# Stick-breaking attention in parts: the running product is turned itself and meets differences of values

## The chip, the cores and the metric

The kernel runs on one core of a Trainium2 chip. Its engines are TensorE (PE in the profile, with its weight loads as PEld), VectorE (DVE), ScalarE (ACT), GpSimd (POOL) and SyncE (SP), which here only issues DMAs. Each engine takes its instructions in the order in which they were written for it and waits at the first one that is not ready. The metric is the device time of one execution in microseconds, as the median over runs.

## The reference

One decoder layer on 2048 tokens of 1024 channels, all in float32: a norm; one input projection to conv value, conv gate, q, k and v; a causal depthwise convolution of width 31 with gate, norm and swish; stick-breaking attention of 8 heads of 64 channels with a norm per head; an output projection; a residual; and a gated feed-forward part. The change touches attention alone. Cut to what it computes:

```python
z = einsum("bhqd,bhkd->bhqk", q, k) / 8
mask = key_pos < q_pos                       # strictly earlier tokens
log_beta = log_sigmoid(z)
log_1m_beta = where(mask, log_sigmoid(-z), 0)
between = cumsum(log_1m_beta, reverse=True) - log_1m_beta
attn = where(mask, exp(log_beta + between), 0)
out = attn @ v
```

Written without logarithms, token t gives to an earlier token s the weight sigmoid(z_ts) times the product of sigmoid(-z_tj) over all j between s and t. Let R_s be the product over all j from s up to the token just before t. Then, as sigmoid(z) = 1 - sigmoid(-z), the weight of s is R_(s+1) - R_s, with R_t = 1.

## The kernel before

**Precision.** A float32 operand is split into a high half (the value rounded to the fast matmul type, written by ACT) and a low half (the rest, a subtraction on DVE or POOL), and a product is two or three matmuls of halves. A "low half" below is such a subtraction (`split`, L592 to L595).

**Stages.** Tokens go in four groups g of 512 (`G`). A list `PLAN` (L40) orders the main stream of PE: input projection of groups 0 to 3 (L602 to L606), output projections (L1030 to L1032) as groups become ready, and the first parts of the feed-forward work (`c11`, `p4`, L1104). Beside this stream run three side streams, each reaching a share of its work at a given point of the main stream: attention, the convolution (31 taps a channel block on DVE, L820) and sums of feed-forward weights on POOL (L1188). When all of these are written, a planner (`Graph`) replaces the written order: it models every instruction with a cost and every buffer with its users, orders each engine's instructions anew, and pins that order. What follows, from about 1460 us on, is the rest of the feed-forward part; it is ordered separately.

**V.** The projection of v for one pair of heads leaves PSUM through ACT into a tile vs, channels by tokens (L777). After the next projection PE turns it in four blocks (L782), the halves are made, and the result goes to DRAM (`vd`). q and k go to DRAM as halves.

**Attention.** A unit is one head and one group of 512 keys; a head of group g has g + 1 units, from the newest keys to the oldest. A unit has four row blocks j of 128 queries. For each, `scores` does this:

- PE: z = QK, two matmuls (L904, L905), into one of two PSUM banks;
- on the newest (diagonal) unit, whose width is (j + 1) x 128, DVE adds -1e30 above the diagonal (L907, 128 x 128);
- POOL copies the carry of the unit before, one column, to the end of tile om (L909), and ACT writes sigmoid(-z) beside it (L910);
- ACT writes sigmoid(z) to tile A (L912);
- DVE replaces om by its running product from right to left, carry first (L914, one element more than the keys);
- POOL multiplies A by om shifted by one (L915), and copies the last product to pv, the next carry (L917).

The scan's second operand is a broadcast that it does not use; it is a column of z in PSUM, except in the last group's heads 4 to 7 (`late`), where it is a column of ones in SBUF.

`values` then takes the unit before the current one, one key block of 128 at a time: PE turns the four row blocks of A (L931), ACT and DVE make the halves TH and TL, and PE adds V times both to the head's sum o (L936, L937). At a head's end ACT copies o to oT (L1001); three quarter-units later PE turns it and DVE adds the two halves (`fold_halves`, L952, L953), and every second head the pair is normalised and turned back (`back`, L969).

Buffers: om has four, A six, z and the turned blocks (at) two PSUM banks each, o and oT one.

## Time and profile before

| | us |
|---|---|
| median of 3 runs | 2450.47 |
| lowest and highest run | 2440.8, 2454.69 |
| the profiled execution, whole | 2447.04 |
| its span, first to last instruction | 2445.3 |

The profile is of one execution. A row of a group of instructions reads: line, engine, operation, output from inputs, shape, count | busy us in all, mean ns of one | idle time of the engine just before them, and what ended most of it. A row of a wait reads: who waited, for whom, us in total, times, longest. A row of a stretch of time gives its length and then, for each engine, busy us and the number of instructions. The first scan starts at 62.2 us and the last one ends before 1380 us, so all that the change touches lies in the first 1400 us. The granted clock of TensorE is 0.993 of full speed over the span.

### The profile page before, as it was taken

What the parts mean: (1) busy time and instruction counts of PE and PEld (TensorE: products, weight loads), DVE (VectorE), ACT (ScalarE), POOL (GpSimd) and SP (SyncE); (2) the same over time, 40 slices, a digit from 0 to 9 for tenths busy, and PEclk for the clock granted to TensorE, in tenths of its full rate; (3) what the DMA queues carried; (4) which work ended last, traced back from release to release, by engine and by line L of the source; (5) the groups of instructions that cost most, each with busy time, mean ns of one, the idle gap of its engine ahead of it and who ended that gap; (6) DMA issues with size and microseconds to landing.
All of it is one profiled execution on the core that took longest, in us unless ns stands there. A gap on an engine that the chain in (4) does not pass through costs nothing. (4 is left out here: it accounts for less than half of the span.)

```text
span 2445.3 us, 35497 instructions
## 1 busy us (share of the span) xinstructions
PE 2360.7 (97%) x11156; PEld 1927.7 (79%) x11156; DVE 1786.1 (73%) x2305; ACT 1295.6 (53%) x2398; POOL 1528.3 (62%) x1845
## 2 busy tenths in 40 slices
PE   8999999999999999998899999999999999999998
PEld 6788887787878777886678877777888887887886
DVE  6997999999997899766751257677656664556656
ACT  4567675776666655666664653333323235454543
POOL 5756477674767667669941147754766665567656
PEclk9999999999999999999999999999999999999999
DMA  9898876888699799875598769878888777668765
GB/s 317 282 317 270 278 233 227 294 282 256 224 298 312 247 340 323 299 258 177 197 339 276 264 223 330 307 263 274 291 293 277 261 253 252 198 190 277 240 192 177
DMA packets 279197, 648.40 MB, mean 265 GB/s; under 512 B 34400, under 2 KB 34400, under 8 KB 279008
## 3 DMA queue, kind: packets, MB, share of 16 engines
q1 hardware_dynamic: 263168, 617.29, 75.6%
q10 hardware_dynamic: 15840, 28.84, 3.1%
q8 instruction: 88, 1.44, 0.2%
q14 instruction: 101, 0.83, 0.1%
HBM read 456.21 MB, written 189.79 MB: 264 GB/s over the span
## 5 line engine op out<-in xcount | busy, mean ns | idle before, releaser
L915 POOL TENSOR_TENSOR A<-A,om 128x512 f32<-128x512 f32 (+2 forms) x320 | 326.8, 1023 | 332.7 <-DVE om L914 249.3
L1398 POOL TENSOR_TENSOR wL<-raw,wH 128x512 fp32r<-128x512 f32 x176 | 254.5, 1469 | 196.5 <-ACT wH L1397 165.4
L820 DVE SCALAR_TENSOR_TENSOR cv<-glu,cw,cv 128x512 f32<-128x512 f32 x464 | 346.8, 747 | 4.7
L1629 DVE TENSOR_TENSOR xL__21922<-t__21924,xH__21921 128x512 fp32r<-128x512 f32 x154 | 198.3, 1293 | 160.7 <-ACT xH__21921 L1628 160.4
L1627 POOL TENSOR_TENSOR xL__21920<-t__21923,xH__21919 128x512 fp32r<-128x512 f32 x154 | 212.0, 1383 | 155.9 <-ACT xH__21919 L1626 152.3
L914 DVE TENSOR_TENSOR_SCAN om<-om,one,z 128x513 f32<-128x513 f32 (+3 forms) x256 | 278.3, 1100 | 16.6 <-ACT A L912 13.6
L595 DVE TENSOR_TENSOR TL<-at,TH 128x512 fp32r<-128x512 f32 (+1 forms) x320 | 188.6, 600 | 122.9 <-ACT TH L594 120.6
L602 PE MATMUL inps<-xH,wL 128*128 128x512 f32 x640 | 258.4, 404 | 3.7 <-ACT sg L769 2.6
L604 PE MATMUL inps<-xH,wH 128*128 128x512 f32 x640 | 256.2, 401 | 0.0
L606 PE MATMUL inps<-xL,wH 128*128 128x512 f32 x640 | 256.1, 400 | 0.0
L1104 PE MATMUL dps<-xH__21919,xL__21922 128*128 128x512 f32 x616 | 240.9, 391 | 3.5 <-DVE xL__21922 L1629 2.7
L1104 PE MATMUL dps<-xL__21920,xH__21921 128*128 128x512 f32 x616 | 240.6, 391 | 1.8 <-POOL xL__21920 L1627 1.8
L1104 PE MATMUL dps<-xH__21919,xH__21921 128*128 128x512 f32 x616 | 240.3, 390 | 0.0
L910 ACT ACTIVATE om<-z 128x512 f32<-128x512 f32 (+2 forms) x320 | 173.1, 543 | 111.5 <-DVE z L907 59.2
L556 ACT ACTIVATE wH<-raw 128x1024 fp32r<-128x1024 f32 x156 | 166.6, 1068 | 117.3 <-PE inps L606 50.3
L931 PE MATMUL at<-idr,A 128*128 128x128 f32 x1088 | 198.2, 274 | 16.0 <-POOL A L915 12.1
L1626 ACT ACTIVATE xH__21919<-t__21923 128x512 fp32r<-128x512 f32 x154 | 97.3, 632 | 217.7 <-POOL xL__21920 L1627 120.2
L594 ACT ACTIVATE TH<-at 128x512 fp32r<-128x512 f32 (+1 forms) x320 | 168.3, 544 | 74.5 <-PE at L931 69.3
L1397 ACT ACTIVATE wH<-raw 128x512 fp32r<-128x512 f32 x176 | 101.2, 623 | 172.5 <-PE b L1104 56.2
L931 PEld LDWEIGHTS at<-idr,A 128*128 128x128 f32 x1088 | 140.1, 140 | 58.2 <-POOL A L915 16.5
L912 ACT ACTIVATE A<-z 128x512 f32<-128x512 f32 (+2 forms) x320 | 173.1, 544 | 17.1 <-PE at L931 17.1
L560 POOL TENSOR_TENSOR wL<-raw,wH 128x1024 fp32r<-128x1024 f32 x50 | 121.3, 2428 | 48.9 <-ACT wH L556 33.5
(292 smaller groups left out, 6324.8 us busy)
## 6 DMA issues: line engine op xcount, KB each, us to landing
wL<-wL SPq DMA_DIRECT2D x156, 512.0 KB, 5.3
raw<-in_w_in_dram SPq DMA_DIRECT2D x80, 512.0 KB, 5.7
t__21924<-u SPq DMA_DIRECT2D x154, 256.0 KB, 2.8
c<-c ACTq DMA_DIRECT2D x88, 256.0 KB, 4.8
t__21923<-wd SPq DMA_DIRECT2D x88, 256.0 KB, 2.9
K<-kd SPq DMA_DIRECT2D x80, 256.0 KB, 4.3
V<-vd SPq DMA_DIRECT2D x80, 256.0 KB, 4.5
u<-accf SPq DMA_DIRECT2D x22, 768.0 KB, 4.8
```

The lines of the kernel that those rows point to most:

```text
L595: nc.vector.tensor_tensor(L, ps, H.bitcast(F32), ALU.subtract)
L602: nc.tensor.matmul(ps, WL[:, kc], aH[t](k), start=k == 0, stop=False)
L604: nc.tensor.matmul(ps, WH[:, kc], aH[t](k), start=False, stop=False)
L606: nc.tensor.matmul(ps, WH[:, kc], aL[t](k), start=False, stop=k == KT - 1)
L820: nc.vector.scalar_tensor_tensor(to, gl[c][:, k:k + G], cw[:, c, k:k + 1], a, ALU.mult, ALU.add)
L914: nc.vector.tensor_tensor_scan(r, r, (one if late else z[:, 0:1]).to_broadcast([P, w + 1]), one, ALU.mult, ALU.bypass)
L915: nc.gpsimd.tensor_tensor(a[:, 0:w], a[:, 0:w], om[:, G - w + 1:G + 1], ALU.mult)
L931: nc.tensor.transpose(pt[:, j * P:(j + 1) * P], u["A"][j][:, b * P:(b + 1) * P], id32)
L1104: return nc.tensor.matmul(ps, a, b, skip_group_check=True, **flags)
L1398: nc.gpsimd.tensor_tensor(l, t, f32(h), sub)
L1627: nc.gpsimd.tensor_tensor(WL, w, f32(WH), sub)
L1629: nc.vector.tensor_tensor(UL, t, f32(UH), sub)
```

## The change

The weights R_(s+1) - R_s are not formed. The sum over s of (R_(s+1) - R_s) v_s is regrouped as the sum over s of R_s (v_(s-1) - v_s), plus v_(t-1). So:

- **scores.** om gets sigmoid(-z) alone, and the scan's running product R is what PE turns later. A, its sigmoid and its multiplication are gone, as are both copies of carries: the scan takes its start value from column 0 of the om tile of the unit before.
- **diagonal.** The mask is gone. The diagonal scan computes (mark + state) x om from right to left with start 0, where `lower` has a single 1 in each row, at the token just before the query: the state stays 0 until there and is the product from there on. Its operands are two SBUF tensors. For row 0 of row block 0 that token lies in the key group before, so for groups 1 to 3 POOL adds the mark to that block's carry (L923 in the new kernel).
- **values.** Unchanged, but the V that is read is the difference of neighbours: POOL makes `step` from vs (one subtraction of 511 columns, one of a single column against the last column of the group before, one copy of that column), and PE turns `step` instead of vs. vs also goes to DRAM, by SP (16 stores of 256 KB).
- **head's end.** v_(t-1) is loaded back for a pair of heads (16 loads) and POOL adds its 64 channels to oT, in either half of the partitions, before the folding.
- **buffers.** om has eight, A none.

```diff
+    lower = ap.tile([P, G], F32, name="lower", bufs=1)
+    nc.gpsimd.memset(lower, 0.0)
+    nc.gpsimd.affine_select(lower, lower, pattern=[[1, G]], compare_op=ALU.not_equal, fill=1.0, base=P + 1 - G,
                             channel_multiplier=-1)
+    vlast = cc.tile([P, 48], F32, name="vlast")
+    nc.gpsimd.memset(vlast, 0.0)
...
                 nc.scalar.activation(vs, ps, AF.Copy)
-
-                def later(c=c, vs=vs):
+                nc.sync.dma_start(vsd[c][:, g * G + 1:(g + 1) * G + 1], vs)
+                step = ev("step")
+                nc.gpsimd.tensor_tensor(step[:, 1:G], vs[:, 0:G - 1], vs[:, 1:G], ALU.subtract)
+                nc.gpsimd.tensor_tensor(step[:, 0:1], vlast[:, c:c + 1], vs[:, 0:1], ALU.subtract)
+                nc.gpsimd.tensor_copy(vlast[:, c:c + 1], vs[:, G - 1:G])
+
+                def later(c=c, vs=step):
...
-            return dict(QH=QH, QL=QL, prev=[one] * TT, o=None)
+            return dict(QH=QH, QL=QL, prev=[lower[:, 0:1]] * TT, o=None)
...
+            om = ap.tile([P, G], F32, tag="om", name="om", bufs=NOM)
+            nc.scalar.activation(om[:, 0:w], z[:, 0:w], AF.Sigmoid, scale=-0.125)
+            r = om[:, 0:w][:, ::-1]
             if diag:
-                nc.vector.tensor_tensor(z[:, w - P:w], z[:, w - P:w], msk, ALU.add)
-            om = ap.tile([P, G + 9], F32, tag="om", name="om", bufs=NOM)
-            nc.gpsimd.tensor_copy(om[:, G:G + 1], hd_["prev"][j])
-            nc.scalar.activation(om[:, G - w:G], z[:, 0:w], AF.Sigmoid, scale=-0.125)
-            a = ap.tile([P, G], F32, tag="A", name="A", bufs=NA)
-            nc.scalar.activation(a[:, 0:w], z[:, 0:w], AF.Sigmoid, scale=0.125)
-            r = om[:, G - w:G + 1][:, ::-1]
-            nc.vector.tensor_tensor_scan(r, r, (one if late else z[:, 0:1]).to_broadcast([P, w + 1]), one, ALU.mult, ALU.bypass)
-            nc.gpsimd.tensor_tensor(a[:, 0:w], a[:, 0:w], om[:, G - w + 1:G + 1], ALU.mult)
-            pv = sp.tile([P, 1], F32, tag="pv", name="pv", bufs=8)
-            nc.gpsimd.tensor_copy(pv, om[:, G - w:G - w + 1])
-            hd_["prev"][j] = pv
-            u["A"].append(a)
+                nc.vector.tensor_tensor_scan(r, lower[:, G - w:G][:, ::-1], r, hd_["prev"][j], ALU.add, ALU.mult)
+            else:
+                nc.vector.tensor_tensor_scan(r, r, (one if late else z[:, 0:1]).to_broadcast([P, w]), hd_["prev"][j],
+                                             ALU.mult, ALU.bypass)
+            hd_["prev"][j] = om[:, 0:1]
+            if w == P and g:
+                hd_["prev"][j] = sp.tile([P, 1], F32, tag="pv", name="pv", bufs=2)
+                nc.gpsimd.tensor_tensor(hd_["prev"][j], om[:, 0:1], lower[:, G - P - 1:G - P], ALU.add)
+            u["A"].append(om)
...
                 nc.scalar.activation(oT, heads[h]["o"], AF.Copy)
+                if h % 2 == 0:
+                    vsh = ap.tile([P, G], F32, tag="vsh", name="vsh", bufs=1)
+                    n = int(g == 0)
+                    if n:
+                        nc.gpsimd.memset(vsh[:, 0:n], 0.0)
+                    nc.sync.dma_start(vsh[:, n:G], vsd[h // 2][:, g * G + n:(g + 1) * G])
+                hp = slice(h % 2 * DH, (h % 2 + 1) * DH)
+                nc.gpsimd.tensor_tensor(oT[hp, :], oT[hp, :], vsh[hp, :], ALU.add)
```

The planner orders all of this anew. Three places show how its order moves. The rows give line, operation, output from inputs and shape; x2 stands for two alike in a row.

GpSimd, where the first low halves of the feed-forward weights (wL of 512 columns) stand between attention of the last group, in the kernel before:

```order
L573 TENSOR_TENSOR wL<-raw,wH 128x512
L915 TENSOR_TENSOR A<-A,om 128x512 x2
L917 COPY pv<-om 128x1 x2
L909 COPY om<-pv 128x1 x2
L1188 TENSOR_TENSOR sum<-sum 128x512
L537 TENSOR_SCALAR ms<-ss 128x1
L538 TENSOR_TENSOR rs<-ms,nhalf 128x1
L573 TENSOR_TENSOR wL<-raw,wH 128x512
L1067 TENSOR_TENSOR big<-big,xr 128x512
L915 TENSOR_TENSOR A<-A,om 128x512 x2
L573 TENSOR_TENSOR wL<-raw,wH 128x512
```

and in the changed one, at the same weights:

```order
L571 TENSOR_TENSOR wL<-raw,wH 128x512
L1201 TENSOR_TENSOR sum<-sum 128x512
L535 TENSOR_SCALAR ms<-ss 128x1
L536 TENSOR_TENSOR rs<-ms,nhalf 128x1
L1201 TENSOR_TENSOR sum<-sum 128x512 x2
L571 TENSOR_TENSOR wL<-raw,wH 128x512
L1080 TENSOR_TENSOR big<-big,xr 128x512 x2
L571 TENSOR_TENSOR wL<-raw,wH 128x512
```

Between two weights attention no longer stands; its products and copies are gone.

VectorE, a head's diagonal unit while the convolution's taps (cv) run, before:

```order
L907 TENSOR_TENSOR z<-z,msk 128x128
L595 TENSOR_TENSOR TL<-at,TH 128x128
L820 SCALAR_TENSOR_TENSOR cv<-glu_134,cw,cv 128x512
L907 TENSOR_TENSOR z<-z,msk 128x128
L820 SCALAR_TENSOR_TENSOR cv<-glu_134,cw,cv 128x512
L914 SCALAR_TENSOR_TENSOR om<-om,one,z 128x129
L914 SCALAR_TENSOR_TENSOR om<-om,one,z 128x257
```

and such a unit in the changed kernel:

```order
L916 SCALAR_TENSOR_TENSOR om<-lower,om 128x128
L593 TENSOR_TENSOR TL<-at,TH 128x128
L826 SCALAR_TENSOR_TENSOR cv<-glu_138,cw,cv 128x512
L916 SCALAR_TENSOR_TENSOR om<-lower,om 128x256
L826 SCALAR_TENSOR_TENSOR cv<-glu_138,cw,cv 128x512
```

The masks are gone, and the scan reads the marks and om, no longer a broadcast of z.

SyncE's queue, where the halves of V are stored, before:

```order
L788 DMA vd_0_159<-vt 128x512
L562 DMA wL_935<-wL 128x1024
L555 DMA raw<-in_w_in_dram 128x1024
L788 DMA vd_0_159<-vt 128x512
L562 DMA wL_983<-wL 128x1024
```

and in the changed kernel:

```order
L794 DMA vd_0_167<-vt 128x512
L553 DMA raw<-in_w_in_dram 128x1024
L779 DMA vs_147<-vs 128x512
L560 DMA wL_896<-wL 128x1024
L899 DMA V<-vd_0_167 128x512
```

The store of the whole vs stands between the loads and stores of projection weights.

More of the change, by code (lines that the diff above doesn't have):

```diff
@@ L35 @@
 EPS = 1e-6
-NEG = -1e30
-NOM = 4
-NA = 6
+NOM = 8
 PLAN = (
@@ L639, in layer_kernel @@
     nc.vector.tensor_copy(idr, ident)
-    msk = cc.tile([P, P], F32, name="msk")
-    nc.gpsimd.memset(msk, NEG)
-    nc.gpsimd.affine_select(msk, msk, pattern=[[1, P]], compare_op=ALU.is_ge, fill=0.0, base=0,
+    lower = ap.tile([P, G], F32, name="lower", bufs=1)
+    nc.gpsimd.memset(lower, 0.0)
+    nc.gpsimd.affine_select(lower, lower, pattern=[[1, G]], compare_op=ALU.not_equal, fill=1.0, base=P + 1 - G,
                             channel_multiplier=-1)
+    vlast = cc.tile([P, 48], F32, name="vlast")
+    nc.gpsimd.memset(vlast, 0.0)
     one = cc.tile([P, 1], F32, name="one")
@@ L655, in layer_kernel @@
     vd = {}
+    vsd = [dp.tile([P, S + 1], F32, name=f"vs{c}") for c in range(CB)]
     for g in range(NG):
```

## The prediction

> **What bounds the kernel now.** I began with the page's first part, because the change takes work off every engine but one.
>
> ```profile
> PE 2360.7 (97%) x11156; PEld 1927.7 (79%) x11156; DVE 1786.1 (73%) x2305; ACT 1295.6 (53%) x2398; POOL 1528.3 (62%) x1845
> ```
>
> TensorE (PE) does 11156 matmuls and transposes before, and the order of the changed kernel has as many, of the same widths: on this engine nothing is saved. Only time in which PE does not stream can be won. The 97% makes that look small, but a matmul's row lasts longer than its turn. The weight loads show the pace better, stage by stage (the columns are stretch, its length, then busy us and count of PE, PEld, DVE, ACT, POOL, then granted clock, DMA share, GB/s):
>
> ```profile
> 100.00:700.00 600.00, 591.74 (x3025) 483.92 (x3024) 574.02 (x874) 399.51 (x775) 390.39 (x672) 0.99 0.81 265
> 850.00:1000.00 150.00, 143.43 (x713) 114.26 (x714) 145.15 (x197) 90.21 (x165) 97.19 (x130) 1.00 0.95 330
> 1000.00:1100.00 100.00, 99.66 (x488) 82.13 (x487) 63.96 (x79) 63.84 (x115) 65.07 (x89) 1.00 0.81 271
> 1100.00:1250.00 150.00, 133.32 (x678) 106.10 (x678) 109.83 (x127) 100.05 (x199) 137.54 (x179) 0.99 0.63 209
> 1850.00:1900.00 50.00, 50.00 (x223) 41.39 (x222) 30.67 (x37) 14.85 (x26) 31.88 (x23) 1.00 0.80 276
> ```
>
> The last row is a stretch of pure feed-forward: 222 matmuls in 50 us, 0.225 us each, loads busy 41.39/50 = 0.828. Against that, 100 to 700 us has 0.807, 850 to 1000 has 0.762, 1100 to 1250 has 0.707 and 1000 to 1100 has 0.821. The loss is about 15, 12, 22 and 1 us. (Attention's transposes are short turns with a load each, so the true loss is somewhat larger.) So two things bind beside PE: VectorE (DVE), 96% and 97% busy in the first two rows, and GpSimd (POOL), 92% busy from 1100 to 1250. The engines that the loads waited for say the same. First the whole execution, then 1050 to 1250 us alone:
>
> ```profile
> PEld at L931 <- POOL A L915: 16.5, 15, 4.3
> PEld z L904 <- DVE om L914: 15.6, 27, 1.9
> PEld o L937 <- DVE TL L595: 9.3, 27, 0.9
> PEld o L936 <- ACT TH L594: 5.5, 11, 1.6
> PEld at L931 <- DVE TL L595: 5.0, 8, 1.4
> PEld po L969 <- DVE ot L961: 3.7, 3, 1.7
> PEld at L931 <- DVE ot L953: 1.8, 2, 1.2
> PEld z L904 <- ACT A L912: 1.6, 3, 0.8
> ```
> ```profile
> PEld at L931 <- POOL A L915: 15.5, 13, 4.3
> PEld at L931 <- DVE TL L595: 2.6, 3, 1.4
> PEld o L937 <- DVE TL L595: 2.4, 5, 0.9
> PEld z L904 <- ACT A L912: 1.6, 3, 0.8
> ```
>
> The eight rows of attention add up to 59.0 us; that is the listed prize. The wait for the product A, the step that the change deletes, is 16.5 us, of which 15.5 lie in the POOL-bound stage and only 1 in the DVE-bound ones. There PE waits for the scan (its read of z holds the bank) and for the low halves TL.
>
> **POOL, deleted and added.** The product and the three kinds of one-column copies go (first two rows whole execution, the rest 1100 to 1250 us):
>
> ```profile
> L915 POOL TENSOR_TENSOR A<-A,om 128x512 f32<-128x512 f32 (+2 forms) x320 | 326.8, 1023 | 332.7 <-DVE om L914 249.3
> L917 POOL COPY pv<-om 128x1 f32<-128x1 f32 x320 | 74.2, 238 | 30.6 <-DVE om L914 30.1
> L909 POOL COPY om<-pv 128x1 f32<-128x1 f32 x192 | 40.5, 219 | 4.8
> L909 POOL COPY om<-one 128x1 f32<-128x1 f32 x128 | 26.1, 215 | 2.5
> ```
> ```profile
> L915 POOL TENSOR_TENSOR A<-A,om 128x512 f32<-128x512 f32 (+3 forms) x39 | 48.6, 1251 | 7.7 <-PE at L931 3.8 <-DVE om L914 2.6 <-PE p L1104 1.3
> L917 POOL COPY pv<-om 128x1 f32<-128x1 f32 x38 | 15.7, 421 | 0.1
> L909 POOL COPY om<-pv 128x1 f32<-128x1 f32 x27 | 6.9, 272 | 0.2
> L909 POOL COPY om<-one 128x1 f32<-128x1 f32 x12 | 4.0, 355 | 0.1
> ```
>
> That is 326.8 + 74.2 + 40.5 + 26.1 = 467.6 us. For what is added, the nearest rows:
>
> ```profile
> L1067 POOL TENSOR_TENSOR big<-big,xr 128x512 f32<-128x512 f32 x24 | 33.2, 1390 | 12.3 <-DVE big L1064 12.2
> L538 POOL TENSOR_TENSOR rstd<-ms,nhalf 128x1 f32<-128x1 f32 x28 | 15.8, 566 | 1.5
> ```
>
> Sixteen steps of V cost 1.39 + 0.57 + 0.24 us each (35), 32 head sums 1.39 (44), 24 corrected carries 0.57 (14): 93 us, a net 374 off POOL. From 1100 to 1250 us 75.2 us go and, with some 2.5 heads ended there, about 5 come: 137.5 becomes 67. POOL stops binding there. The wait on A becomes a wait on the scan, which stood ahead of it anyway. Of the 22.1 us in the short list I take **18**; the bounds are 8 (the scan takes the place of POOL for half of it) and 22.
>
> **DVE: masks out, scans dearer.** The masks cost 36.3 us in all, 25.2 of them in the two DVE-bound rows:
>
> ```profile
> 100.00:700.00 600.00, 22.86 (x80) 0.99 0.81 265
> 850.00:1000.00 150.00, 2.30 (x8) 1.00 0.95 330
> ```
>
> The diagonal scan now reads two SBUF tensors (the marks and the sigmoids), where it read one from SBUF and one broadcast from PSUM. Both kinds stand in the trace, since half the heads of the last group already scan without PSUM. The first five rows are the whole execution, the sixth 1100 to 1250 us:
>
> ```profile
> L914 DVE TENSOR_TENSOR_SCAN om<-om,one,z 128x513 f32<-128x513 f32 x172 | 217.7, 1274 | 14.2 <-ACT A L912 11.4 <-POOL om L909 1.9 <-POOL acc L851 0.2
> L914 DVE TENSOR_TENSOR_SCAN om<-om,one 128x513 f32<-128x513 f32 x52 | 81.1, 1572 | 39.7 <-ACT om L910 38.4 <-POOL om L909 0.7 <-POOL pv L917 0.4
> L914 DVE TENSOR_TENSOR_SCAN om<-om,one,z 128x385 f32<-128x385 f32 x28 | 28.3, 1012 | 1.5 <-ACT A L912 1.3
> L914 DVE TENSOR_TENSOR_SCAN om<-om,one,z 128x257 f32<-128x257 f32 x28 | 20.7, 740 | 0.5 <-ACT A L912 0.4
> L914 DVE TENSOR_TENSOR_SCAN om<-om,one,z 128x129 f32<-128x129 f32 x28 | 13.4, 478 | 0.4 <-ACT A L912 0.4
> L914 DVE TENSOR_TENSOR_SCAN om<-om,one 128x513 f32<-128x513 f32 x30 | 49.0, 1647 | 11.2 <-ACT om L910 10.0 <-POOL om L909 0.7 <-POOL pv L917 0.4
> ```
> ```profile
> L914 DVE TENSOR_TENSOR_SCAN om<-om,one x64: 474/1287/2357, 1048.6 to 1376.1; 128x513 f32<-128x513 f32 x52, 128x129 f32<-128x129 f32 x4, 128x257 f32<-128x257 f32 x4, 128x385 f32<-128x385 f32 x4
> ```
> ```profile
> 100.00:700.00 600.00, 172.77 (x163) 0.99 0.81 265
> ```
>
> (The last two are the scans without PSUM, with shortest, median and longest ns, and all scans from 100 to 700 us.)
>
> So without PSUM a full scan takes 1647 instead of 1274 ns, 29% more, where POOL is 92% busy; the excess should follow POOL's load. From 100 to 700 us 163 of 320 scans run, so POOL falls from 390 by half of 467.6 and gains half of 93: about 200 of 600, a third: 29% x 33/92 is about 10%. The 128 diagonal scans take (28.3 + 20.7 + 13.4) x 32/28 + 32 x 1.274 = 112 us; 88 of them, 77 us, lie in the two rows, so 8 us are lost. DVE is relieved by 25 - 8 = **17** us there, and as it has no idle time to speak of, I count all of it. Bounds: 25.2 with no collision, 3 with the full 29%.
>
> The Trainium skill ("SBUF — State Buffer", section "Who interferes with whom") says that a VectorE instruction with two SBUF inputs and a GpSimd instruction that reads SBUF exclude each other for a whole instruction. The 1274 against 1572 ns agree with that, and it speaks against this one edit; how far it could go is the last rival.
>
> **ACT.** One sigmoid of two goes:
>
> ```profile
> L912 ACT ACTIVATE A<-z 128x512 f32<-128x512 f32 (+2 forms) x320 | 173.1, 544 | 17.1 <-PE at L931 17.1
> ```
>
> 173.1 us less on an engine that is 67% busy at most in these stages. Its own share of the 59 us is TH 5.5 outside and inside the stage above; I take **3** of it (bounds 0 and 5). The eight buffers of om replace six of A and four of om; four of them are held by the unit that is being turned, so four instead of two stand free for the unit being scanned. The 17.1 us that ACT waited for transposes before writing A were that shortage; they are ACT's, covered by its idle time, and count nothing here.
>
> **What is added on the path.** (1) V's transposes now wait for POOL's step, some 2.2 us after the copy from PSUM. Behind a late transpose stand all of PE's matmuls. All 16 exposed would be 35 us; no V transpose is among the waits now, the order leaves projection matmuls between, and POOL is freer: 1. (2) 16 stores and 16 loads of 256 KB on SP's queue, ahead of weight loads:
>
> ```profile
> K<-kd SPq DMA_DIRECT2D x80, 256.0 KB, 4.3
> ```
>
> 8.4 MB at the 330 GB/s of the 850-to-1000 row would be 25 us if DMA set the pace. None of PE's attention waits is for a DMA: 1, bounds 0 and 25. (3) The head sum stands between the copy of o and the folding transposes, 1.4 us on three quarter-units of distance; the carry of row block 0 still takes POOL's 0.6 us where it took 0.24 + 0.22: 1 together. Sum **3**.
>
> **Sum.** 18 + 17 + 3 - 3 = 35 us off the profiled execution's 2447.04 (span 2445.3 and 1.7 around it): 2412. The runs' median is 2450.47, 3.4 above that execution, inside their own spread of 14; I say **2413**. The case's own range is 2398 to 2432.
>
> **Rivals.** *All the listed waiting goes* (0.20): the shorter chain and a freer POOL and ACT also clear the waits for z and TL elsewhere. Then 59 us less the 3 added give -56: 2391. For it: the DVE relief of 17 comes on top of shorter latencies. Against: DVE stays near 93% busy from 100 to 700 us ((574 - 17)/600).
> *The wait changes its name* (0.20): DVE gives its 17 us to convolution taps, which already fill every gap, and PE waits at the turn for the scan. Then only the low 8 of the POOL stage is won, less 3: 2442. For it: POOL's own waiting was 249.3 us for the scan, so POOL was mostly behind DVE. Against: from 1100 to 1250 us DVE is 73% busy.
> *Diagonal scans blocked by POOL* (0.10): each of them waits for a running POOL instruction. The longest scan took 2357 against 1274 ns, so up to 1.08 us. At a mean of 0.7 us the 88 scans cost 62 - 25 = 36 us in the DVE-bound stages, against 18 won and 3 paid: +21, 2468. It turns the sum to slower from (25.2 + 18 - 3)/88 = 0.46 us a scan. Against: the mean excess was 0.3 to 0.37 us under a POOL twice as busy. The lock of which the Trainium skill speaks, above, would be its mechanism; the means bear it out only at that smaller price.
>
> **Chances.** The forecast 0.50, the rivals 0.20, 0.20 and 0.10. A change under 0.5% (12 us, 2438 to 2463) can't be told from none here. Faster: 0.50 + 0.20 + a quarter of the second rival = 0.75; same 0.15; slower 0.10. Range 2372 to 2450: it takes in the first two rivals with the unknowns (all of the DMA's 25 or much of V's 35 exposed brings 2412 to about 2440; the first rival with the relief of 17 beside it 2391 to 2374), and leaves the blocked scans out.
>
> **What would show it.** PE waits at the turn in 1050 to 1250 us under 5 us and POOL near 67 of 150 there; POOL about 1150 and ACT about 1120 us in all; diagonal full scans of 1300 to 1450 ns; load shares of about 0.83 from 100 to 700 and above 0.78 from 1100 to 1250; the part behind 1500 us unchanged. A wait on the scan of 15 us or more at the turn, or diagonal scans above 1.8 us, would make it wrong; so would waits of PE for V's step or for DMA.

## The result, and the profile after

The changed kernel takes 2429.65 us (median of 4 runs, 2429.04 to 2429.93); the kernel before took 2450.22 us on the same chip (4 runs, 2440.8 to 2454.69). The ratio is 0.9921, with a 95% interval of 0.9892 to 0.9950: 19.4 us faster, interval 12 to 26. A second set of runs gave 2428.9 us (ratio 0.9935, 0.9916 to 0.9953). The forecast was 2413, so about half of the 35 us came. Whether it came for the reasons of the forecast is what the rest of the document is about, and the answer is: one of its two large terms did, and the size of the total owes much to the order in which the planner put the work.

The page's first part, kernel after:

```profile
PE 2353.6 (97%) x11156; PEld 1929.4 (79%) x11156; DVE 1766.3 (73%) x2177; ACT 1163.8 (48%) x2078; POOL 1196.0 (49%) x994
```

POOL lost 332 us, ACT 132 and DVE 20; PE has the same 11156 instructions. DVE lost less than its masks alone (36.3 us). (This line counts time in which two instructions of an engine overlap once, the rows of single groups count it twice: ACT's rows before add up to 1454 us where this line has 1296. The rows of ACT fell by 180 us, those of POOL by 367.) The stages, kernel after (stretch, length, busy us and count of PE, PEld, DVE, ACT, POOL, granted clock, DMA share, GB/s):

```profile
0.00:100.00 100.00, 81.92 (x365) 65.95 (x366) 70.63 (x96) 42.37 (x69) 49.00 (x58) 0.97 0.88 286
100.00:700.00 600.00, 586.93 (x3012) 482.35 (x3011) 564.32 (x792) 334.29 (x609) 244.17 (x247) 1.00 0.83 271
1100.00:1250.00 150.00, 146.45 (x754) 119.00 (x753) 110.87 (x119) 92.02 (x174) 94.25 (x78) 1.00 0.85 286
```

From 1100 to 1250 us PE loads 753 times where it loaded 678 times, and POOL is busy for 94 of 150 us instead of 138. From 100 to 700 us nothing is won: 3011 loads, before 3024. The first 100 us, which the prediction did not quote, got worse. The same stretch of the kernel before:

```profile
0.00:100.00 100.00, 86.34 (x399) 69.81 (x400) 75.27 (x119) 49.53 (x86) 56.06 (x87) 1.00 0.94 313
```

A cut at 850 and 1400 us puts it into two numbers. First the kernel before, then the kernel after:

```profile
0.00:850.00 850.00, 825.68 (x4177) 674.66 (x4177) 774.01 (x1167) 546.19 (x1045) 547.15 (x924) 1.00 0.83 273
850.00:1400.00 550.00, 523.16 (x2550) 423.01 (x2551) 353.20 (x440) 335.00 (x607) 327.81 (x437) 0.99 0.81 275
```
```profile
0.00:850.00 850.00, 816.32 (x4121) 670.12 (x4122) 758.16 (x1052) 457.20 (x819) 351.92 (x372) 0.99 0.84 276
850.00:1400.00 550.00, 541.20 (x2674) 441.59 (x2673) 356.57 (x434) 300.41 (x525) 191.14 (x140) 1.00 0.86 295
```

One turn of PE takes 850/4177 = 0.2035 us here. By 850 us the changed kernel has 55 loads fewer: it is 11 us behind. From 850 to 1400 us it does 122 more: 25 us won. That leaves 14 of the 17 us by which the two profiled spans differ (2445.3 and 2428.1). Counting turns in this way is used below for every kernel; it holds because they all give PE nearly the same work.

The five longest waits of the weight loads from 1050 to 1250 us, kernel after (us in total, times, longest):

```profile
PEld at L936 <- DVE TL L593: 3.0, 5, 1.0
PEld pf L957 <- POOL oT L1014: 2.0, 1, 2.0
PEld z L910 <- ACT om L913: 1.4, 4, 0.8
PEld o L942 <- DVE TL L593: 1.0, 2, 0.7
PEld at L936 <- DVE om L918: 0.5, 1, 0.5
```

The 15.5 us for the product A are gone, and the scan (last row, 0.5 us) has not taken their place.

### The profile page after: what moved, and what is told of

It is laid out like the page before. It is cut to its first block, busy times and chain, and to the rows that moved or that the text cites. A ratio compares the mean times of both kernels' runs of the same rounds, so it can differ in the third digit from the quotient of the medians.

```text
span 2428.1 us, 33643 instructions
## 1 busy us (share of the span) xinstructions
PE 2353.6 (97%) x11156; PEld 1929.4 (79%) x11156; DVE 1766.3 (73%) x2177; ACT 1163.8 (48%) x2078; POOL 1196.0 (49%) x994
## 5 line engine op out<-in xcount | busy, mean ns | idle before, releaser
L936 PE MATMUL at<-idr,om 128*128 128x128 f32 x1088 | 185.4, 273 | 7.2 <-DVE TL L593 2.7
L936 PEld LDWEIGHTS at<-idr,om 128*128 128x128 f32 x1088 | 136.8, 140 | 48.0 <-DVE TL L593 6.3
L1201 POOL TENSOR_TENSOR sum<-sum 128x512 f32<-128x512 f32 x88 | 124.6, 1416 | 100.2 <-DMA sum<-in_w_up_dram 40.3
L918 DVE TENSOR_TENSOR_SCAN om<-om,z 128x512 f32<-128x512 f32 x124 | 156.8, 1271 | 8.5 <-ACT om L913 8.2
L600 PEld LDWEIGHTS inps<-xH,wL 128*128 128x128 f32 x640 | 121.7, 190 | 34.5 <-ACT sg L770 5.8
```

The costliest lines, as they stand in the source:

```text
L600: nc.tensor.matmul(ps, WL[:, kc], aH[t](k), start=k == 0, stop=False)
L936: nc.tensor.transpose(pt[:, j * P:(j + 1) * P], u["A"][j][:, b * P:(b + 1) * P], id32)
```

## The experiments

### The product alone, in the old order

Both kernels get their order from a planner, so any edit moves everything else too. To price one term by itself the order must stand still. Here the kernel before multiplies only every 32nd column of A (so most of the weights are left out of attention), while the planner is told the old width; every engine's instructions stay in their old places.

```
-            nc.gpsimd.tensor_tensor(a[:, 0:w], a[:, 0:w], om[:, G - w + 1:G + 1], ALU.mult)
+            m = nc.gpsimd.tensor_tensor(a[:, 0:w:32], a[:, 0:w:32], om[:, G - w + 1:G + 1:32], ALU.mult)
+            FAKE[m.ins.name] = w
```

> The kernel before with the product A on every 32nd column alone (the rest of the weights is left out, so the result is another), the planner told the old width: exactly the order of the kernel before, with 250 to 300 us less on POOL and a shorter link in the chain. Theory, POOL bound 1050 to 1250 us: the waits for A go, 15 to 20 us are won there and next to nothing before 1000 us: 2425 to 2432 us. Rival, POOL's products also hold up the scans on DVE elsewhere: below 2420 us. Rival, the new order and not the deleted work made the changed kernel faster: above 2440 us.

Measured: 2424.15 us, ratio 0.9908 (0.9890 to 0.9926), 23 us less, 1 us beyond the expected range. The product's group, three stretches, and what is left of the wait for A from 1050 to 1250 us:

```profile
L918 POOL TENSOR_TENSOR A<-A,om 128x16 f32<-128x16 f32 (+2 forms) x320 | 98.5, 308 | 477.0 <-DVE om L917 360.3 <-ACT A L915 41.4 <-PE at L935 28.1
```
```profile
0.00:850.00 850.00, 826.72 (x4194) 678.01 (x4195) 769.61 (x1173) 548.32 (x1052) 400.20 (x928) 1.00 0.84 275
850.00:1400.00 550.00, 540.27 (x2646) 440.95 (x2647) 351.55 (x448) 344.17 (x622) 237.95 (x436) 1.00 0.85 288
1100.00:1250.00 150.00, 145.81 (x745) 118.74 (x744) 108.85 (x129) 110.81 (x215) 108.42 (x188) 0.99 0.80 266
```
```profile
PEld at L935 <- POOL A L918: 0.8, 2, 0.4
```

The product fell from 326.8 to 98.5 us, POOL from 138 to 108 of the 150 us, and PE does 96 loads more from 850 to 1400 us (20 us) and 18 more before (4 us). From 1050 to 1250 us alone, the stretch from which the forecast took its 18 us, the wait for A fell from 15.5 to 0.8 us, and the loads rise from 915 to 986: 14 us. Thinning one instruction of the 467.6 us that the change takes off POOL is thus worth as much as the whole change (the intervals of the two overlap). The stage was bound by POOL, as the forecast said; whether by POOL's load or by the product as a link of the chain this run can't separate, as it shortens both. The run with more load, below, does.

### The mask alone, in the old order

The kernel before with a mask of 8 columns for 128 (the mask is incomplete, so masked places get weight), the planner told 128.

```
-                nc.vector.tensor_tensor(z[:, w - P:w], z[:, w - P:w], msk, ALU.add)
+                m = nc.vector.tensor_tensor(z[:, w - 8:w], z[:, w - 8:w], msk[:, P - 8:P], ALU.add)
+                FAKE[m.ins.name] = P
```

> The kernel before with the mask on 8 instead of 128 columns (so most of the mask is left out and the result is another), while the planner is told the old width: every engine has exactly the order of the kernel before, and DVE loses about 120 x 1.04 = 125 ns for each of 128 masks, 16 us in all, some 11 us of it in the DVE-bound stages. If work on DVE there is on the path, the time falls by 5 to 11 us, to 2436 to 2442 us, although leaving the mask out with a new order was 9 us slower. If it is not on the path, 2446 to 2449 us.

Measured: 2442.86 us (10 runs), ratio 0.9986 (0.9975 to 0.9996): 3.4 us less by the ratio, 4.3 by the medians; this lies between the two expected ranges, nearer to the first.

```profile
L910 DVE TENSOR_TENSOR z<-z,msk 128x8 f32<-128x8 f32 x128 | 20.4, 166 | 10.5 <-PE z L908 10.3
```

The masks cost 20.4 us here and 36.3 before. So 15.9 us off DVE bring about 4 (by the interval 1 to 6). 10.9 of the 15.9 lie in the two DVE-bound rows, which the forecast counted in full: less than half of them came. DVE at 96% busy was not what PE waited for most of the time. The waits that are listed tell more: those of PE's loads for the scan and for TL, the rows of 15.6, 9.3 and 5.0 us in the kernel before, are 13.5, 7.3 and 4.4 us here, 4.7 less in all.

### The diagonal scan with one operand in PSUM

In the changed kernel the sigmoid of a diagonal unit is written back over its scores in PSUM, so the scan reads one tensor from SBUF and one from PSUM.

```
-            nc.scalar.activation(om[:, 0:w], z[:, 0:w], AF.Sigmoid, scale=-0.125)
+            nc.scalar.activation(z[:, 0:w] if diag else om[:, 0:w], z[:, 0:w], AF.Sigmoid, scale=-0.125)
...
-                nc.vector.tensor_tensor_scan(r, lower[:, G - w:G][:, ::-1], r, hd_["prev"][j], ALU.add, ALU.mult)
+                nc.vector.tensor_tensor_scan(r, lower[:, G - w:G][:, ::-1], z[:, 0:w][:, ::-1], hd_["prev"][j],
+                                             ALU.add, ALU.mult)
```

> On diagonal units alone the sigmoid is written back into its PSUM bank and the scan reads it there, so that it has one SBUF input and not two. If the two SBUF inputs are why diagonal scans take 583, 861, 1254 and 1430 ns, they fall to about 480, 740, 1010 and 1275, DVE loses 20 us in all, and the stages before 1000 us gain 5 to 12 us: 2418 to 2425 us. If the collision doesn't set the end (DVE's taps fill the room), the scans are faster and the time is the same, 2428 to 2432 us. If the bank held longer matters, PE waits for z and it is slower.

The diagonal scans grouped by shape, kernel after and then this one (last numbers: busy us, mean ns, idle before):

```profile
L916 DVE TENSOR_TENSOR_SCAN om<-lower,om 128x512 f32<-128x512 f32 x32 | 45.8, 1430 | 2.3 <-ACT om L913 2.3
L916 DVE TENSOR_TENSOR_SCAN om<-lower,om 128x384 f32<-128x384 f32 x32 | 40.1, 1254 | 0.3 <-ACT om L913 0.3
L916 DVE TENSOR_TENSOR_SCAN om<-lower,om 128x256 f32<-128x256 f32 x32 | 27.5, 861 | 0.9 <-ACT om L913 0.7
L916 DVE TENSOR_TENSOR_SCAN om<-lower,om 128x128 f32<-128x128 f32 x32 | 18.7, 583 | 6.6 <-ACT om L913 6.6
```
```profile
L916 DVE TENSOR_TENSOR_SCAN om<-lower,z 128x512 f32<-128x512 f32 x32 | 40.5, 1267 | 3.0 <-ACT z L913 2.9
L916 DVE TENSOR_TENSOR_SCAN om<-lower,z 128x384 f32<-128x384 f32 x32 | 32.2, 1005 | 2.4 <-ACT z L913 2.4
L916 DVE TENSOR_TENSOR_SCAN om<-lower,z 128x256 f32<-128x256 f32 x32 | 23.5, 735 | 0.1
L916 DVE TENSOR_TENSOR_SCAN om<-lower,z 128x128 f32<-128x128 f32 x32 | 15.1, 473 | 13.5 <-ACT z L913 13.5
```

132.1 us with both tensors in SBUF, 111.3 with one: the collision with POOL costs 20.8 us, 19%, not the 10% of the forecast. With the operand moved, the scans fell to the durations of the kernel before. And yet the kernel became slower than the changed one: 2437.42 us, ratio 0.9962 (0.9947 to 0.9977). Its largest single wait is 9.0 us, behind a subtraction that took 10.7 us for 0.69 (shortest, median and longest ns of twelve):

```profile
PEld o L943 <- DVE TL L593: 15.8, 13, 9.0
```
```profile
L874 DVE TENSOR_TENSOR xL<-ma,xH x12: 665/686/10746, 355.9 to 1067.0; 128x512 fp32r<-128x512 f32 x12
```

The same subtraction took 9.3 us in one execution of the changed kernel, which then needed 2437.49 us (below). That is about as much as this kernel lost in its profiled execution (2439.44); whether the subtraction was as slow in its other three runs is not on record. A cost of the edit itself (z's bank is held until the scan ends) is thus not shown.

### V's own buffer, and no token ahead

In the changed kernel PE stands still for 5 us near 52 us, while the kernel before has no stand above 2 there. V's copy vs and its step use the shared "ev" buffers; the first of two runs gives vs a buffer of its own (om then has 7 for 8).

```
-                vs = ev("vs")
+                vs = ap.tile([P, G], F32, tag="vs", name="vs", bufs=1)
```

> The changed kernel, correct as it is, but v's tile vs is taken out of the shared buffers into one of its own, paid with one of the eight buffers of om (7). The shared buffers then have as many tenants as in the kernel before. If the shortage of shared buffers is what lost the start, the 5 us stand is gone and the time is 2415 to 2423 us. If the eighth om buffer is worth more, it is above 2430 us.

The second leaves out the value ahead: vs isn't stored or read back, and nothing is added to the heads (attention's output lacks that term).

```
-                nc.sync.dma_start(vsd[c][:, g * G + 1:(g + 1) * G + 1], vs)
...
-                if h % 2 == 0:
-                    vsh = ap.tile([P, G], F32, tag="vsh", name="vsh", bufs=1)
...
-                    nc.sync.dma_start(vsh[:, n:G], vsd[h // 2][:, g * G + n:(g + 1) * G])
...
-                nc.gpsimd.tensor_tensor(oT[hp, :], oT[hp, :], vsh[hp, :], ALU.add)
```

> The changed kernel without the token ahead: no store of v to DRAM, no load back, no head sum (its attention lacks v_(t-1), so the result is another; the steps of V stay). In the changed kernel's profile ACT waits 3.3 us at 56 us for a DMA before it may write the second half tile vt, with the sigmoid that PE needs behind it, and PE stands still for 5 us there. If that DMA is the store of v, which holds one of the four shared buffers (ev) until it has landed, the wait goes and with the freed buffers the first 200 us lose about 32 us instead of 42: 2415 to 2422 us. If the store and the sums cost nothing, 2427 to 2432 us.

Measured: 2434.05 us (0.9950, 0.9930 to 0.9971) and 2431.18 us (0.9941, 0.9923 to 0.9959). The own buffer shortened the stand to 3.0 us, with V's transposes at 49.3 us where they are at 51.9 in the changed kernel. Its first 100 us are nearly those of the kernel before (397 loads against 400):

```profile
0.00:100.00 100.00, 87.03 (x396) 70.04 (x397) 69.02 (x99) 46.24 (x75) 51.59 (x60) 0.98 0.92 302
```

It lost that again later, 5.4 us of it in one wait for the subtraction of L874, which took 6.7 us here. So the place of the transposes, the buffers, or both can account for the stand; this run changes both and doesn't separate them. Without stores, loads and sums the stand is still 4.9 us, so the store of vs doesn't make it, and the time is that of the changed kernel within 2 us. The order moved with this edit too, so a cost of a few us can't be excluded. In the changed kernel no wait of PE's loads for a DMA is listed, and one of 2.0 us for the head sum (above).

### More load on POOL, and the mask gone from the kernel before

To the changed kernel, products on POOL that nothing reads, over the same columns as the product that was deleted:

```
+            jk = ap.tile([P, 2 * P], BF16, tag="jk", name="jk", bufs=1)
+            for q in range(0, w, 2 * P):
+                e = min(q + 2 * P, w)
+                nc.gpsimd.tensor_tensor(jk[:, 0:e - q], om[:, q:e], om[:, q:e], ALU.mult)
```

> The changed kernel plus, for each row block, a product of the finished scan with itself into a small tile that nobody reads (pieces of at most 256 columns, so about 1.4 us for a full row block where the deleted product took 1.17): POOL's work is back, but nothing of attention waits for it except the release of om. Theory 1, POOL's load bounded 1100 to 1250 us: the waiting comes back there (POOL over 85% busy, weight loads near 0.72 of the stage) and 15 to 20 us are lost: 2445 to 2450 us. Theory 2, the link through POOL in the chain was what cost: hardly a change, 2430 to 2435 us.

Measured: 2468.61 us, ratio 1.0091 (1.0075 to 1.0108). POOL's stage, this kernel, and one of its waits over the whole execution:

```profile
1100.00:1250.00 150.00, 133.86 (x649) 107.26 (x648) 102.40 (x109) 76.30 (x145) 135.07 (x136) 0.98 0.66 217
```
```profile
PEld p L1121 <- POOL wL L571: 10.2, 6, 4.2
```

With POOL at 135 of 150 us again, PE is back at 648 loads there, though nothing of attention reads the product (om's buffers alone wait for it): 8.3 of the 10.2 us for the low halves of the feed-forward weights lie in this stage. So POOL's load is enough to bind it. The signs are those of the first theory, the time is not: it lies 19 us above its range, and above the kernel before. The added products cost POOL 394 us where the deleted one cost 327, and the order is a third one; how much is due to which stays open.

And the kernel before without its mask (masked places get weight), planned anew:

```
-            if diag:
-                nc.vector.tensor_tensor(z[:, w - P:w], z[:, w - P:w], msk, ALU.add)
```

> The kernel before without the mask on diagonal blocks (it leaves out the mask, so a query also reads itself and later tokens of its block): 36 us less on DVE, everything else as before. If DVE's relief is worth what I counted (25 us in the DVE-bound stages, all of it on the path) the time falls by 15 to 25 us to 2425 to 2435 us. If taps and scans only move up and PE waits as before, it falls by under 8 us.

Measured: 2456.63 us, ratio 1.0041 (1.0026 to 1.0056). Taking 36 us off DVE made the kernel 9 us slower, which neither expectation allowed, while 16 us off in the old order made it 4 us faster. After this the order itself was the suspect.

### The same work in other orders

Four kernels whose work is that of the changed kernel, or of the one before, instruction for instruction. In the first the planner believes that V's step takes 1 ns, and so places V's transposes earlier.

```
+                m = nc.gpsimd.tensor_tensor(step[:, 1:G], vs[:, 0:G - 1], vs[:, 1:G], ALU.subtract)
+                FAKE[m.ins.name] = 1
+                m = nc.gpsimd.tensor_tensor(step[:, 0:1], vlast[:, c:c + 1], vs[:, 0:1], ALU.subtract)
+                FAKE[m.ins.name] = 1
```

> The changed kernel with one thing told otherwise to the planner: V's two step instructions (the long one of 511 columns and the first column) are planned as if they took 1 ns. They are still executed at full length, so nothing of the computation changes; only the order does, and V's transposes are placed about five matmul groups earlier in TensorE's row. Theory 'V's longer chain costs the start' (the 5.06-us stand of TensorE near 52 us in the changed kernel, 2.07 us in the kernel before, and 6.8 us of half clock behind it): the transposes come early enough that the bank they hold is given back sooner, the stand falls to about 2 to 3 us, no half clock behind it, and the time comes to 2420 to 2425. Theory 'the place was luck of the order': the stand may go or stay, and the time lies anywhere within 10 us of 2429, the early gain being given back in other places. Theory 'the step itself is too slow for its place': V's transposes now wait 1 to 2 us for POOL in each of 16 tiles in the place of the stand, and the time is 2430 to 2440.

In two others the planner's assumed DMA rate is moved by 0.3%, and in the last the kernel before gets the first of these.

```
-RATE, ISSUE, AHEAD, LAND = 350.0, 450.0, 700.0, 5000.0
+RATE, ISSUE, AHEAD, LAND = 349.0, 450.0, 700.0, 5000.0
```

> The changed kernel with one constant of the planner moved by 0.3% (the assumed DMA rate, 349 for 350). The work is the same instruction for instruction; only the order moves. Theory 'the order alone is worth some 8 us': the time lies 3 to 10 us off 2429, on either side. Rival 'the order hardly matters when the work is the same': within 2 us of 2429, and then what the first experiments lost (8 us with shorter scans, 9 us with the mask gone) must be a cost of their edits.

> As the run with 349, with 351 for 350: the changed kernel's work in a third order. Theory 'the order alone is worth some 8 us': 3 to 10 us off 2429, not by the same amount as with 349. Rival 'the order hardly matters': within 2 us of 2429.

> The kernel before with the same constant at 349 for 350: its work in another order. Theory 'the order alone is worth some 8 us': 3 to 10 us off 2448, and the change with both kernels planned at 349 is then worth anything from 10 to 35 us. Rival 'the order hardly matters': 2446 to 2450, and the difference of the two kernels at 349 is again 18 to 22.

| work | order | us | ratio to before (95%) | loads by 850 us | loads 850 to 1400 us |
|---|---|---|---|---|---|
| changed | its own | 2429.65 | 0.9921 (0.9892 to 0.9950) | 4122 | 2673 |
| changed | V's step as 1 ns | 2453.18 | 1.0023 (1.0008 to 1.0039) | 4086 | 2631 |
| changed | rate 349 | 2459.19 | 1.0051 (1.0036 to 1.0066) | 4054 | 2620 |
| changed | rate 351 | 2448.08 | 1.0001 (0.9990 to 1.0012) | 4115 | 2631 |
| before | its own | 2447.62 | 1 | 4177 | 2551 |
| before | rate 349 | 2448.53 | 1.0006 (0.9996 to 1.0015) | 4139 | 2573 |

(The 2447.62 of the kernel before is the median of 23 runs beside the four new kernels, on another chip than the runs above, where the kernel before took 2447.1 to 2447.4; the changed kernel in its own order was not run there. Within one order the runs spread too: V's step as 1 ns took 2446 to 2459 us, rate 351 2442 to 2454. The profiled executions of these two were 4 and 6 us under their medians.) The stretches of the four, in the table's order of the new runs, first V's step as 1 ns, then 349, 351, and the kernel before at 349:

```profile
0.00:850.00 850.00, 811.10 (x4085) 663.53 (x4086) 752.30 (x1039) 455.09 (x815) 350.47 (x373) 0.99 0.84 275
850.00:1400.00 550.00, 535.04 (x2632) 437.79 (x2631) 368.09 (x439) 296.85 (x514) 187.47 (x136) 0.99 0.85 287
```
```profile
0.00:850.00 850.00, 807.59 (x4053) 662.14 (x4054) 750.77 (x1031) 454.21 (x811) 340.19 (x370) 0.98 0.84 273
850.00:1400.00 550.00, 531.86 (x2621) 433.44 (x2620) 365.00 (x439) 290.28 (x503) 192.92 (x139) 1.00 0.84 284
```
```profile
0.00:850.00 850.00, 814.18 (x4114) 668.40 (x4115) 759.76 (x1048) 457.79 (x819) 355.33 (x375) 1.00 0.85 277
850.00:1400.00 550.00, 534.62 (x2632) 435.22 (x2631) 361.81 (x432) 295.28 (x514) 191.54 (x136) 1.00 0.83 287
```
```profile
0.00:850.00 850.00, 822.54 (x4138) 670.49 (x4139) 764.73 (x1156) 540.77 (x1034) 545.04 (x917) 0.99 0.83 272
850.00:1400.00 550.00, 526.66 (x2573) 428.45 (x2573) 363.18 (x448) 336.60 (x611) 328.76 (x445) 0.99 0.81 274
```

The same work takes 2430 to 2459 us, depending on its order; that is more than the change itself. The expected 3 to 10 us were far too few: the changed kernel moved by 24, 30 and 18 us. At 349 in both kernels the change makes it 11 us slower, where 10 to 35 us faster was expected. That the changed kernel is 19 us faster is a property of the one order that its planner found; over these four orders its work is not faster on the whole than that of the kernel before. Not all of the spread is the planner's, though: with rate 349 some 10 us go to one slow subtraction (last section). In every one of the four orders the changed kernel wins from 850 to 1400 us (69 to 122 loads over the kernel before, 14 to 25 us), and in every one it is behind at 850 us (55 to 123 loads, 11 to 25 us). Of the three new orders one ends where the kernel before does, one 6 us behind and one 12 us behind. The kernel before lost 38 loads by 850 us (8 us) to another order and won 22 back: its measured time moved by only 1 us.

Part of the early loss has a cause that can be pointed at. The longest single wait from 40 to 75 us in the kernel before, in the kernel after, and with V's step planned as 1 ns:

```profile
PEld inps L602 <- POOL wL L560: 1.9, 1, 1.9
```
```profile
PEld inps L600 <- issue: 4.9, 1, 4.9
```
```profile
PEld inps L605 <- issue: 3.6, 1, 3.6
```

and the first 100 us of the latter:

```profile
0.00:100.00 100.00, 86.12 (x394) 69.93 (x395) 69.88 (x101) 46.05 (x75) 51.26 (x60) 1.00 0.91 302
```

With V's transposes placed earlier the start is that of the kernel before: 395 loads (before 400, after 366), clock 1.00 (after 0.97). So of the 7 us lost in the first 100 us of the changed kernel most come from where V's longer chain (copy, POOL's step, transposes, copies) puts its transposes. The run with V's own buffer, whose transposes came earlier too, agrees. The price varies: the changed kernel's second execution has 374 loads there, the orders with 349 and 351 have 384 and 383, with single waits of 4.4 and 4.3 us, so it is 3 to 7 us. The expected gain in the total did not follow (2453 us lies in the range of none of the three theories): this order loses 86 loads (17 us) between 100 and 850 us, the changed kernel's own order only 21 (its 55 less the 34 of the first 100 us). A third of the 17 us is the step itself, for which the transposes now wait in the stretch from 100 to 850 us:

```profile
PEld vps L795 <- POOL step L788: 6.1, 6, 1.6
```

That is the third theory's wait, in 6 of 16 tiles. The other 11 us lie scattered over waits of 1 to 3 us for VectorE and ScalarE; which edit or which place in the order they go back to stays open.

### The same kernel again

The changed kernel, unchanged:

> The changed kernel once more, for a second profile of it on the chip of the other three. If the loss at the start (12 us more waiting of PE in the first 200 us than in the kernel before, among it one single wait of 4.9 us that the profile puts down to issue) belongs to the order of the changed kernel, it stands here again and the time is 2428 to 2431 us. If it was an accident of that execution, the wait is gone and 0 to 200 us holds about 30 us of lost turns instead of 42.

Measured: 2428.9 us, ratio 0.9935 (0.9916 to 0.9953), one run of four at 2437.49. That one was profiled, and it shows in one row why. The subtraction of L874, 12 times, with shortest, median and longest ns: first the earlier execution (2429.93 us), then this one:

```profile
L874 DVE TENSOR_TENSOR xL<-ma,xH x12: 678/690/1783, 367.9 to 1060.1; 128x512 fp32r<-128x512 f32 x12
```
```profile
L874 DVE TENSOR_TENSOR xL<-ma,xH x12: 674/684/9298, 366.0 to 1069.0; 128x512 fp32r<-128x512 f32 x12
```

One instruction of 0.68 us took 9.3. More of this in the last section.

## Why the prediction was right, and where it was not

- **The POOL stage, 18 us (bounds 8 and 22): right.** The fixed-order run gives 14 us of it from 1050 to 1250 us, 20 from 850 to 1400 and 23 in all; the changed kernel's four orders give 14 to 25 from 850 to 1400. The wait for A is gone, and the scan took 0.5 us of it. POOL stands at 94 of 150 us, not 67: the forecast took the product out but did not see that the stage, being faster, takes in more of the other work. Head sums and carries were dear enough (44.3 us and 8.2) but hidden, but for one wait of 2.0 us.
- **The DVE relief, 17 us (bounds 3 and 25): wrong, and this is the step that failed.** Two things in it. The collision of the diagonal scans was put at 10%, 8 us on the 88 scans of those stages; it is 19%, 20.8 us on all 128 or by their share about 14 on the 88, so DVE is relieved there by some 11 us, not 17. And "as it has no idle time to speak of, I count all of it" doesn't hold: in the old order 15.9 us less DVE, 10.9 of them in those stages, were worth about 4. By this measure the term should have been 4.
- **ACT, 3 us: not priced apart.** The waits for TH fell from 5.5 to 2.8 us; ACT's total is 1164, not 1120, although all of the sigmoid's 173 us went and no other group grew by more than 0.2 us: the forecast took a row's busy time off a total that counts overlapping time once. For the same reason POOL shows 1196 and not 1150; its rows fell by 367 us, against 374 forecast.
- **Added on the path, 3 us: too small.** DMA shows no wait, and sum and carry one of 2.0 us, for 1 and 1. V's chain costs 7 us in the first 100 us of this order, not as waits at the transposes (one wait of 1.0 us for the step in the whole execution) but by moving them, and with them the copy that frees the bank.
- **What was in no term: the order.** With +20 for POOL, +4 for DVE and -7 for V's chain the sum is 17, the measured difference of the two profiled spans (17.2). That agreement is luck as far as the runs show: the other orders of the same work give 12 us more to 5 us less than the kernel before in their profiled spans. A forecast from the work alone can't be better than some 15 us here. That the result lay within the predicted range (2372 to 2450) is in part luck: two of the three other orders of the same work lie above it, at 2453 and 2459.
- **The rivals.** "All the listed waiting goes" fell: 2391 was not neared. "The wait changes its name" fell in the POOL stage, but its first half stands in the main: most of DVE's microseconds went to nothing that PE waits for. The sign that it named, a wait of 15 us on the scan at the turn, did not come: the rows with the scan at the turn add up to 6.4 us over the whole execution. "Diagonal scans blocked by POOL" was right in kind and too dear: the mean excess was 0.16 us a scan (20.8/128), not 0.7; its point of decision was 0.46. The signs named ahead: load shares 0.804 (482.35/600) and 0.793 (119.00/150) against "0.83" and "above 0.78"; full diagonal scans 1430 ns against 1300 to 1450. The first share is no higher than before (0.807), which speaks against the DVE term.

## What to carry to other kernels

Where a planner sets the order, an edit has two prices, that of the work and that of the new order: measure the first with the order held (shrink the instruction and tell the planner its old size), and measure the second by planning the same work with a constant moved by a hair. A difference between two re-planned kernels that is smaller than the spread of such orders (here 30 us of 2440) says little of the work. And a busy share does not price an engine's microseconds, but the waits of the bottleneck for it come near. With the order held, 15.9 us off an engine at 96% brought 4 us and 90 us off POOL from 850 to 1400 us brought 20: about a quarter both times. What came back was in both cases near what the loads waited less: 4.7 us for DVE, 15.7 us for A.

## What was not expected of the hardware

**A VectorE instruction passed over for 9 us.** In the order with rate 349 the worst single loss stands at 400 us. The timeline there, VectorE and then GpSimd (start, us, instruction, times):

```profile
400.91 9.73 DVE L874 TENSOR_TENSOR xL<-ma,xH 128x512 fp32r<-128x512 f32 x1
410.56 0.68 DVE L958 TENSOR_REDUCE ot<-pf 128x256 f32<-128x512 f32 x1
```
```profile
398.97 9.90 POOL L713 TENSOR_TENSOR xcol<-xcol,rb 128x512 f32<-128x512 f32 x8
408.84 1.25 POOL L1201 TENSOR_TENSOR sum<-sum 128x512 f32<-128x512 f32 x1
```

The subtraction reads two tensors from SBUF; the median of its twelve is 0.68 us. It began within POOL's unbroken row of eight products and ended 0.5 us behind the next POOL instruction, so it waited through seven or eight of them and not through one. PE stood for 8.9 us behind it:

```profile
PEld at L936 <- DVE ot L958: 9.1, 2, 8.9
```

The Trainium skill ("SBUF — State Buffer", section "Who interferes with whom") says that a VectorE instruction with two SBUF inputs contends with a GpSimd instruction that reads SBUF, and that whoever issues first keeps the shared ports for its whole instruction. The traces agree on the pair, and they add that the loser can be passed over again by the GpSimd instructions that follow. This is read from the timelines: no run moved an operand of this subtraction to PSUM, as one did for the diagonal scans. It is a matter of chance: in the changed kernel's first profile two such subtractions ran beside the same row of POOL products in 2.4 us together, and in its second one of the two took 9.3 us, 8.6 more than its median, which is enough for the 7.6 us between these two spans (2428.1 and 2435.7). The run with the scan's operand in PSUM had one of 10.7 us and that with V's own buffer one of 6.7. It holds for a scan too: with V's step planned as 1 ns a full scan with both operands in SBUF took 6.05 us for 1.25, and POOL's instructions follow each other with no gap until 1150.31 us, 1.1 us before the scan ends; that is about its own length. The timeline there, VectorE and GpSimd:

```profile
1145.34 6.05 DVE L925 TENSOR_TENSOR_SCAN om<-om,pv,one 128x512 f32<-128x512 f32 x1
```
```profile
1144.24 2.32 POOL L576 TENSOR_TENSOR wL<-raw,wH 128x512 fp32r<-128x512 f32 x1
1146.53 2.54 POOL L1087 TENSOR_TENSOR big<-big,xr 128x512 f32<-128x512 f32 x2
1149.03 1.28 POOL L1208 TENSOR_TENSOR sum<-sum 128x512 f32<-128x512 f32 x1
```
The change makes POOL's rows of such products freer to run unbroken, with nothing of attention between them; that this is why instructions held up for 6 us and more show in the changed kernels and not in the five profiles of the kernel before and its variants (longest of this subtraction 2.5 us) is likely, but was not tried.

**A long stand of PE leaves half a clock behind it.** With rate 349 the granted clock fell during the 8.9 us. The stretch from 395 to 425 us, changed kernel in its own order, then with rate 349, and of the latter the 10 us around the end of the stand:

```profile
395.00:425.00 30.00, 29.85 (x149) 24.05 (x148) 29.79 (x41) 14.62 (x25) 24.79 (x17) 1.00 0.58 183
```
```profile
395.00:425.00 30.00, 21.30 (x98) 17.04 (x96) 28.23 (x26) 10.35 (x18) 17.13 (x12) 0.83 0.33 114
```
```profile
405.00:415.00 10.00, 3.70 (x14) 3.32 (x15) 9.01 (x7) 1.80 (x3) 5.09 (x5) 0.50 0.00 0
```

A mean of 0.83 over 30 us is 10 us at half clock, from 405 to 415 us. But 6 of them lie within the stand, which ends at 411.3 us: there PE does nothing. About 4 remain behind it, and half of these, 2 us, are lost. Together that is what the loads show: 96 for 148, 52 turns, 10.6 us. The subtraction that was passed over thus accounts for two fifths of the 123 loads by which this order is behind at 850 us. The 4.9-us stand near 52 us costs more in this way, as its half clock begins only when the stand is nearly over: matmuls of 512 columns start 0.43 us apart from 57.2 to 63.3 us and 0.23 us apart after, so 3 us are lost behind it. The Trainium skill ("TensorE: Matmul & The Clock Gate", Part 1) describes a clock that halves after an idle window of about 3.4 us. The length of a stand alone doesn't decide it here: the stand of 3.6 us (V's step as 1 ns) has a clock of 1.00 in its first 100 us, and behind that of 3.0 us (V's own buffer) matmuls start 0.43 us apart from 55.3 to 58.3 us.
